# Modulation-map products on TensorE in four groups of 32 output partitions, in place of multiply-adds on VectorE

## The chip, the cores and the metric

The kernel runs on one core of one Trainium2 chip. The metric is the device time of one execution in microseconds, the median of several. The engines are called by the profile's names: PE is TensorE (PEld its weight loads), DVE is VectorE, ACT is ScalarE, SP is SyncE, on whose queue nearly all transfers are issued.

## The reference

One inference step of a two-layer backbone over 512 latent and 128 context tokens of 1024 features. Each layer is a feed-forward sub-layer, a token mixer (attention in layer 0, a gated recurrence in layer 1) and a second feed-forward sub-layer. Each of these sub-layers is shifted, scaled and gated by vectors that come from a linear map of a conditioning vector; this map is what the change touches:

```
mod_ctx_all = jnp.einsum('d,lde->le', jax.nn.silu(c_ctx), w_mod) + b_mod
mod_lat_all = jnp.einsum('bd,lde->lbe', jax.nn.silu(c), w_mod) + b_mod[:, None]
# w_mod: (2 layers, 1024, 9 * 1024)
...
mod = mod_lat_all[l].reshape(Bs, N_MOD, D_MODEL)
x = ffn_sublayer(x, mod, 0, norm_g[l, 0], norm_g[l, 1], ffn_w_in[l, 0], ffn_w_out[l, 0])
# ada_pre: rmsnorm(x, g) * (1 + scale) + shift;  ada_post: x + res_w * gate * rmsnorm(y, g)
```

So two vectors of 1024 (latent and context) are multiplied with 2 x 1024 x 9216 weights.

## The kernel before

All activations are held transposed, features on partitions, tokens on the free axis, in two groups g of 320 tokens. The main products run in `run_jobs` (L301): a job is one block of 128 output features over up to eight 128-deep steps, for one or both groups. Every weight is split into a high and a low part (`convert`, L241: ACT copies at L249, DVE subtracts at L250), and each step issues per group two 128x320 matmuls at L315 and one at L320. Weights arrive in three raw buffers (`ensure_dma`, L226, issued at L231 on SP's queue).

Everything else is written as Python generators in the list `bg`. `step_bg` (L281) advances the first of them by one `yield`; `run_jobs` calls it in slots between the steps of a job and once after it, so a generator's work is spread between main matmuls, and the number of its yields fixes its place in the program. The program is then given to a planner of the tile framework, which orders the instructions of each engine by priority (that is, program order) and by when it believes their inputs ready, and places all semaphore waits. It can draw an instruction forward where it believes the engine idle.

The modulation map is computed in 36 blocks of 512 columns. `startup` (L641) makes four of them (0 to 3) with products at L722; the other 32 are made by `mod_gen` (L599), run as a generator in three feed-forward stages: 12 blocks in the first sub-layer of layer 0 (gap 2), 12 in its second (gap 2), 8 in the first of layer 1 (gap 3), as `ffn_jobs` is called in `plan`. A block's weights come in two halves of 512 rows (`mod_load`, L554, issued at L559, two buffers named wmod, one DMA of 1 MB each).

In `mod_gen` before, for each of the eight 128-row steps k and each of the two vectors s, DVE multiplies a 128x512 tile by the scalar `CV[:, k, s]` and adds it into `macc` (L614 for k = 0, L616 for the others), with `gap` yields ahead of each. After step 3 and step 7 the load of the next block's half is issued. Then four matmuls (L626) of 128x256 with a column of ones sum `macc` over the partitions into four groups of 32 output partitions of an accumulator bank (`aux_tile`, two buffers of 128x1024), with the one column placed so that block i falls into rows 2i and 2i+1. ACT copies (i = 0, L631) or DVE adds (L633) the result into `ms`, and after the last block `mod_fin` (L562) brings it into place with four matmuls against `sel` (L567).

In `startup` a block is instead made by eight matmuls of the 128x32 slice of `CS` (zeros but for the two vectors in columns 2 and 3) with 128x512 of the weights, step k into output group k % 4, accumulating over halves and two blocks (L722).

Between sub-layers `chain_gen` (L469) runs the statistics and normalisations that hand one over to the next, on DVE and ACT, with small matmuls at L365 and L377; it uses the same two accumulator buffers.

Of the kernel before, what the change touches and what calls it, by code (L numbers as in the profile page):

```python
# [9 lines left out]
F32 = mybir.dt.float32  # L10
# [3 lines left out]
AF = mybir.ActivationFunctionType  # L14
ALU = mybir.AluOpType
# [4 lines left out]
KT = D // 128  # L20
# [129 lines left out]
class Net:  # L150
# [25 lines left out]
    def setup(self):  # L176
        tc, ctx = self.tc, self.ctx
        P = lambda n, b, **k: ctx.enter_context(tc.tile_pool(name=n, bufs=b, **k))
        self.const = P("const", 1)
        self.big = P("big", 1)  # L180
        self.rawp = P("rawp", RAW_BUFS)
        self.hlp = P("hlp", HL_BUFS)
        self.np_ = P("nrm", 3)
        self.small = P("small", 2)
        self.aux = P("aux", 2, space=PSUM)
        self.mm = P("mm", 1, space=PSUM)
        self.lane = 0
        self.in_attn = False
        big = self.big
        self.Y = [big.tile([128, KT, NG], F32, name="Y0"), None]  # L190
        self.X = big.tile([128, KT, NTOK], F32, name="X")
        self.H = big.tile([128, 2, KT, NTOK], F32R, name="H")
        c = self.const
        self.ident = c.tile([128, 128], F32, name="ident")
        self.sel = c.tile([128, 3, 32], F32, name="sel")
        self.CV = c.tile([128, KT, 2], F32, name="CV")
        self.one = c.tile([128, 64], F32, name="one")
        self.ones = c.tile([128, 1], F32, name="ones")
        self.MODF = c.tile([128, DEPTH * NMOD * KT, 2], F32, name="MOD")
        self.MOD = self.MODF.rearrange("p (l n) s -> p l n s", l=DEPTH)  # L200
        self.NGt = c.tile([128, 96], F32, name="NGt")
        self.BM = c.tile([128, 144], F32, name="BM")
        self.DT = c.tile([128, 50], F32, name="DT")
        self.PRE = c.tile([128, DEPTH, 3, KT, 2], F32, name="PRE")
        self.POST = c.tile([128, DEPTH, 3, KT, 2], F32, name="POST")
        self.acc = {}
        for g in range(2):
            self.acc[g] = c.tile([128, NG], F32, name=f"acc{g}")
        self.lam = c.tile([128, 1], F32, name="lam")
        self.lb = c.tile([128, 2, 16], F32, name="lb")  # L210
        self.again = c.tile([128, 1], F32, name="again")
# [370 lines left out]
    def mod_derive(self, l, p, k0=0, k1=KT):  # L582
# [11 lines left out]
        else:  # L594
            nc.vector.scalar_tensor_tensor(
                out=self.POST[:, l, j, k0:k1], in0=m, scalar=1.0 if j == 1 else 0.5, in1=gv, op0=ALU.mult, op1=ALU.mult
            )

    def mod_gen(self, first, n, gap):  # L599
        nc = self.nc  # L600
        ms = self.mod_p.tile([128, 256], F32, name="ms", tag="ms")
        ts = [self.mod_load(first, h) for h in range(2)]
        for _ in range(MOD_DELAY):
            yield
        for i in range(n):
            acc = [self.mod_p.tile([128, 512], F32, name="macc", tag=f"macc{s}") for s in range(2)]
            for k in range(KT):
                w = ts[k // 4][:, k % 4, :]
                for s in range(2):
                    for _ in range(gap):  # L610
                        yield
                    cv = self.CV[:, k, s:s + 1]
                    if k == 0:
                        nc.vector.tensor_scalar(out=acc[s], in0=w, scalar1=cv, scalar2=None, op0=ALU.mult)  # L614
                    else:
                        nc.vector.scalar_tensor_tensor(  # L616
                            out=acc[s], in0=w, scalar=cv, in1=acc[s], op0=ALU.mult, op1=ALU.add
                        )
                if k % 4 == 3 and i + 1 < n:
                    ts[k // 4] = self.mod_load(first + i + 1, k // 4)  # L620
            yield
            ps = self.aux_tile()
            for g in range(4):
                h, s = divmod(g, 2)
                o = 32 - (2 * i + s)
                nc.tensor.matmul(  # L626
                    out=ps[g * 32:(g + 1) * 32, 0:256], lhsT=self.one[:, o:o + 32],
                    rhs=acc[s][:, h * 256:(h + 1) * 256], start=True, stop=True, skip_group_check=True,
                )
            if i == 0:  # L630
                nc.scalar.activation(out=ms, in_=ps[:, 0:256], func=AF.Copy)  # L631
            else:
                nc.vector.tensor_tensor(out=ms, in0=ms, in1=ps[:, 0:256], op=ALU.add)  # L633
            yield
        yield
        self.mod_fin([(first, n)], ms, self.aux_tile(), True)
        for p in range(first // 2, (first + n) // 2):
            self.mod_derive(*divmod(p, NMOD))
        yield

    def startup(self):  # L641
        nc = self.nc
# [3 lines left out]
        self.open("start", "right", st_p=1)  # L646
        self.open("gs", "left", gs_p=1)
        S = self.st_p
        CS = S.tile([128, KT, 34], F32, name="CS")
        nc.sync.dma_start(out=self.ident, in_=A["k_ident"])  # L650
        rows = {}
        for nm, n in (("D", 50), ("A", 96), ("B", 72), ("C", 72)):
# [12 lines left out]
        for tb in range(5):  # L665
# [4 lines left out]
            src = A["x_sample"][0, tb * 128:(tb + 1) * 128, :] if tb < 4 else A["x_prompt"][0]  # L670
            nc.sync.dma_start(out=t, in_=src)
            xs.append(t)
        nc.vector.memset(CS, 0.0)
        nc.vector.memset(self.one, 0.0)
        nc.vector.memset(self.one[:, 32:33], 1.0)
        nc.vector.memset(self.ones, 1.0 / D)
        loads = []
        for c in (0, 2):
            ts = [self.gs_p.tile([128, 4, 512], F32, name=f"wm{c}{h}") for h in range(2)]
# [3 lines left out]
        ts = [y.rearrange("p k t -> p (k t)")[:, 0:2048].rearrange("p (k c) -> p k c", c=512) for y in self.Y]  # L683
        loads.append([self.mod_load(3, h, ts[h]) for h in range(2)])
        self.ensure_dma(RAW_BUFS - 1)
        ps = self.aux_tile()
# [3 lines left out]
            out=self.CV.rearrange("p k s -> p s k"),  # L690
            in_=self.DT[:, 32:48].rearrange("p (s k) -> p s k", s=2), func=AF.Silu,
        )
        nc.vector.tensor_copy(CS[:, :, 2:4], self.CV)
        ps = self.aux_tile()
        nc.tensor.transpose(ps[:, 0:96], rows["A"], self.ident[0:96, 0:96])
        nc.tensor.transpose(ps[:, 128:200], rows["B"], self.ident[0:72, 0:72])
# [3 lines left out]
        for kt in range(KT):  # L700
            ps = self.aux_tile()
# [8 lines left out]
            out=self.again, in0=self.DT[:, 48:49], scalar1=1.0 - LAM_INIT, scalar2=None, op0=ALU.mult  # L710
        )
        for half in range(2):
            if half == 0:
                for g in BOTH:
                    next(self.first_gens[g])
            ms = self.Y[half].rearrange("p k t -> p (k t)")[:, 2048:2560]
            ps = self.bank()
            for i in range(2):
                ts = loads[2 * half + i]
                for k in range(KT):  # L720
                    g = k % 4
                    nc.tensor.matmul(  # L722
                        out=ps[g * 32:(g + 1) * 32, :], lhsT=CS[:, k, 2 - 2 * i:34 - 2 * i],
                        rhs=ts[k // 4][:, k % 4, :], start=(i == 0 and k < 4), stop=(i == 1 and k >= 4),
                        skip_group_check=True,
                    )
            nc.scalar.activation(out=ms, in_=ps[:, 0:512], func=AF.Copy)
            if half == 0:
                for g in BOTH:
                    for _ in range(STAT_GAP):  # L730
                        next(self.first_gens[g])
            self.mod_fin([(half, 1), (2 + half, 1)], ms, self.bank(), False)
            self.mod_derive(0, 1, 4 * half, 4 * half + 4)
# [688 lines left out]
```

## Time and profile before

| what | value |
|---|---|
| median of 3 runs | 2908.82 us (2905.07 to 2910.05) |
| profiled execution | span 2910.1 us, its own time by the slowest run 2910.05 us |
| PE busy | 2855.3 us, 98%, 19278 matmul records |
| PEld busy | 2749.4 us, 94% |
| DVE busy | 1738.7 us, 60% |
| ACT busy | 995.4 us, 34% |
| DMA | 278.06 MB, mean 96 GB/s |
| mean granted TensorE clock | 0.989 of full speed |

The page gives busy times of one profiled execution. PE's matmuls overlap in their pipeline, so its busy time counts when it has any work; the distance between the starts of matmuls tells its speed. A matmul of two fp32 operands is recorded as two matmuls; the main ones at L315 and L320 use the split form and are one record each. A granted clock of 1.00 is 2.4 GHz and 0.50 is 1.2 GHz.

### The profile page before, as it was taken

Reading aid. Unit: us, or ns where it says so; the run is one execution under the profiler, and the core shown is the slowest. Engines: PE = TensorE matmul, PEld = TensorE weight load, DVE = VectorE, ACT = ScalarE, POOL = GpSimd, SP = SyncE. Lnnn points to the kernel's source line nnn. Section 1 sums busy time; section 2 is a strip of 40 time slices with the busy share of each in tenths; the row PEclk is TensorE's granted clock in tenths of the full one; section 3 lists DMA queues with packets and bytes.
Section 4 is the critical chain, followed back from the end, with each engine's and each line's share of the span. In section 5 each row is a group of like instructions: output and inputs, shape, how many; then the busy total and the mean of one; then the engine's idle time right before and its main releaser. Section 6 shows DMA issues by size and latency. Waiting matters only on the chain.

```text
span 2910.1 us, 46502 instructions
## 1 busy us (share of the span) xinstructions
PE 2855.3 (98%) x19278; PEld 2749.4 (94%) x19278; DVE 1738.7 (60%) x3605; ACT 995.4 (34%) x1949; POOL 0.2 (0%) x4
## 2 busy tenths in 40 slices
PE   7999999999999999999999999999999999999998
PEld 5999999888888999999999999999999999999998
DVE  6755645866677855665773554387677677223334
ACT  4222123455564422212332212243333344222233
POOL 0000000000000000000000000000000000000000
PEclk9999999999999999999999999999999999999999
DMA  8544432211113344454233433321121122222231
GB/s 264 169 152 139 137 106 81 59 34 36 44 50 101 95 139 151 124 159 138 80 115 104 130 104 107 89 60 55 55 59 51 55 61 80 80 80 73 79 87 39
DMA packets 424399, 278.06 MB, mean 96 GB/s; under 512 B 8410, under 2 KB 385788, under 8 KB 424188
## 3 DMA queue, kind: packets, MB, share of 16 engines
q1 hardware_dynamic: 423680, 274.89, 31.5%
q8 instruction: 152, 2.49, 0.3%
q14 instruction: 59, 0.48, 0.1%
q10 hardware_dynamic: 508, 0.20, 0.0%
HBM read 270.34 MB, written 4.72 MB: 95 GB/s over the span
## 4 chain that ended last, share of the span: by engine, by line
PE 91%; DVE 4%; ACT 2%; issue 1%; DMA 1%; ACTq 0%; DVEq 0%; SPq 0%
PE mmps L315 53%; PE mmps L320 26%; PE aux L1258 2%; PE aux L1067 2%; PE aux L1065 1%; PE mmps L1097 1%; PE aux L377 1%; PE aux L626 1%; PE mmps L1086 1%; ACT sq L1329 1%; PE aux L1295 0%; PE aux L365 0%; DVE whl L250 0%; DVE acc L399 0%; DVE rs_a L358 0%
## 5 line engine op out<-in xcount | busy, mean ns | idle before, releaser
L315 PE MATMUL mmps<-H,whl 128*128 128x320 f32 x7232 | 1447.0, 313 | 8.3 <-ACT H L454 6.1
L315 PEld LDWEIGHTS mmps<-H,whl 128*128 128x128 f32 x7232 | 1159.9, 189 | 26.1 <-issue 8.0
L320 PE MATMUL mmps<-H,whl 128*128 128x320 f32 x3616 | 898.0, 312 | 0.3 <-DVE whl L250 0.3
L250 DVE TENSOR_TENSOR whl<-wraw,whl 128x1024 fp32r<-128x1024 f32 (+1 forms) x324 | 387.7, 1197 | 424.0 <-ACT whl L249 422.7
L320 PEld LDWEIGHTS mmps<-H,whl 128*128 128x128 f32 x3616 | 626.3, 189 | 3.0 <-DVE whl L250 0.6
L249 ACT ACTIVATE whl<-wraw 128x1024 fp32r<-128x1024 f32 (+1 forms) x324 | 335.7, 1038 | 594.5 <-issue 369.0
L315 PE MATMUL mmps<-G,whl 128*128 128x320 f32 x2368 | 467.8, 311 | 1.2 <-ACT G L1343 1.2
L315 PEld LDWEIGHTS mmps<-G,whl 128*128 128x128 f32 x2368 | 378.2, 188 | 6.1 <-issue 3.3
L616 DVE SCALAR_TENSOR_TENSOR macc<-wmod,CV,macc 128x512 f32<-128x512 f32 x448 | 307.6, 746 | 0.0
L320 PE MATMUL mmps<-G,whl 128*128 128x320 f32 x1184 | 294.3, 310 | 0.0
L315 PE MATMUL mmps<-G,H 128*128 128x320 f32 x960 | 216.5, 312 | 0.0
L748 ACT ACTIVATE sa<-mmps 128x320 f32<-128x320 f32 x176 | 69.1, 435 | 427.9 <-PE mmps L320 427.8
L753 DVE TENSOR_TENSOR gm<-sa,mmps 128x320 f32<-128x320 f32 x176 | 79.2, 484 | 217.2 <-PE mmps L320 216.5
L320 PEld LDWEIGHTS mmps<-G,whl 128*128 128x128 f32 x1184 | 204.5, 188 | 0.1
L315 PEld LDWEIGHTS mmps<-G,H 128*128 128x128 f32 x960 | 160.7, 188 | 0.5
L320 PE MATMUL mmps<-G,H 128*128 128x320 f32 x480 | 149.7, 312 | 0.0
L837 DVE TENSOR_TENSOR Y<-Y,mmps 128x320 f32<-128x320 f32 x144 | 66.7, 484 | 133.3 <-PE mmps L320 133.3
L315 PE MATMUL mmps<-H,G 128*128 128x320 f32 x448 | 103.4, 312 | 0.0
L835 ACT ACTIVATE Y<-mmps 128x320 f32<-128x320 f32 x96 | 38.5, 435 | 180.3 <-PE mmps L320 180.0
L399 DVE TENSOR_TENSOR acc<-acc,sq 128x320 f32<-128x320 f32 x168 | 80.2, 487 | 20.3 <-ACT sq L398 18.9
L320 PEld LDWEIGHTS mmps<-G,H 128*128 128x128 f32 x480 | 90.3, 188 | 0.4
L997 DVE TENSOR_REDUCE sm<-aux 128x1 f32<-128x640 f32 x64 | 52.7, 824 | 53.9 <-PE aux L1067 53.8
(222 smaller groups left out, 2540.3 us busy)
## 6 DMA issues: line engine op xcount, KB each, us to landing
wraw<-in_ffn_w_in SPq DMA_DIRECT2D x192, 512.0 KB, 3.9
wmod<-in_w_mod SPq DMA_DIRECT2D x66, 1024.0 KB, 5.6
wraw<-in_ffn_w_out SPq DMA_DIRECT2D x64, 448.0 KB, 3.9
wraw<-in_hgrn_w_in SPq DMA_DIRECT2D x40, 512.0 KB, 3.9
wraw<-in_ffn_w_out SPq DMA_DIRECT2D x32, 512.0 KB, 4.1
wraw<-in_attn_w_in SPq DMA_DIRECT2D x24, 512.0 KB, 4.0
wm<-in_w_mod SPq DMA_DIRECT2D x4, 1024.0 KB, 11.5
wraw<-in_attn_w_out SPq DMA_DIRECT2D x8, 512.0 KB, 4.1
```

The source lines that it names most:

```text
L249: nc.scalar.activation(out=u.w[0][:, 0:nk, :], in_=u.raw[:, 0:nk, :], func=AF.Copy)
L250: nc.vector.tensor_tensor(out=u.w[1][:, 0:nk, :], in0=u.raw[:, 0:nk, :], in1=u.w[0][:, 0:nk, :].bitcast(F32), op=ALU.subtract)
L315: nc.tensor.matmul(out=ps[g][:, 0:NG], lhsT=w[0][:, a, :], rhs=rhs[:, r, b, g * NG:(g + 1) * NG], start=(i == 0 and r == 0), stop=False,)
L320: nc.tensor.matmul(out=ps[g][:, 0:NG], lhsT=w[1][:, a, :], rhs=rhs[:, 0, b, g * NG:(g + 1) * NG], start=False, stop=(i == last),)
L399: return lambda: nc.vector.tensor_tensor(out=acc, in0=acc, in1=sq, op=ALU.add)
L616: nc.vector.scalar_tensor_tensor(out=acc[s], in0=w, scalar=cv, in1=acc[s], op0=ALU.mult, op1=ALU.add)
L748: nc.scalar.activation(out=st[g], in_=ps, func=AF.Silu)
L753: nc.vector.tensor_tensor(out=t, in0=st[g], in1=ps, op=ALU.mult)
L837: nc.vector.tensor_tensor(out=y, in0=y, in1=ps, op=ALU.add)
L997: nc.vector.tensor_reduce(out=sm[:, c:c + 1], in_=x, axis=AX.X, op=ALU.max)
L1067: nc.tensor.matmul(out=o, lhsT=QL[r, qc], rhs=KH[r, c, k0:k1], start=False, stop=True)
L1258: nc.tensor.matmul(out=ps[:, c * 128:(c + 1) * 128], lhsT=km[:, c * 128:(c + 1) * 128], rhs=self.view(Q2, c * 128, dims), start=True, stop ...
```

## The change

`mod_gen` no longer uses DVE for the products. It builds its own `CS` (62 columns per step k, zeros but for the two vectors in columns 30 and 31), and for each half of a block, after 8 x gap yields, issues four matmuls of 128x512 into the four groups of 32 output partitions of one accumulator bank (`mod_rows`); the second half accumulates onto the first. The slice of `CS` shifts by two columns a block, so that block i falls into rows 2i and 2i+1. The load of the next block's half follows each half's products. `ms` is 512 columns wide instead of 256, and `mod_fin` selects sums of all four groups. The number of yields of a block stays the same (16 x gap + 2). `startup` uses the same helpers; the tile of ones (`one`) goes, and the memset of `CS` there is issued after the transposed vectors are at hand.

```diff
-        self.one = c.tile([128, 64], F32, name="one")
...
+    def mod_vectors(self, CS):
+        self.nc.vector.memset(CS, 0.0)
+        self.nc.vector.tensor_copy(CS[:, :, 30:32], self.CV)
+
+    def mod_rows(self, ps, CS, ts, i, half, first, last):
+        for k in range(4 * half, 4 * half + 4):
+            g = k % 4
+            self.nc.tensor.matmul(
+                out=ps[g * 32:(g + 1) * 32, 0:512], lhsT=CS[:, k, 30 - 2 * i:62 - 2 * i], rhs=ts[half][:, g, :],
+                start=first and half == 0, stop=last and half == 1, skip_group_check=True,
+            )
+
     def mod_gen(self, first, n, gap):
         nc = self.nc
-        ms = self.mod_p.tile([128, 256], F32, name="ms", tag="ms")
+        ms = self.mod_p.tile([128, 512], F32, name="ms", tag="ms")
+        CS = self.mod_p.tile([128, KT, 62], F32, name="CS", tag="CS")
+        self.mod_vectors(CS)
         ts = [self.mod_load(first, h) for h in range(2)]
         for _ in range(MOD_DELAY):
             yield
         for i in range(n):
-            acc = [self.mod_p.tile([128, 512], F32, name="macc", tag=f"macc{s}") for s in range(2)]
-            for k in range(KT):
-                w = ts[k // 4][:, k % 4, :]
-                for s in range(2):
-                    for _ in range(gap):
-                        yield
-                    cv = self.CV[:, k, s:s + 1]
-                    if k == 0:
-                        nc.vector.tensor_scalar(out=acc[s], in0=w, scalar1=cv, scalar2=None, op0=ALU.mult)
-                    else:
-                        nc.vector.scalar_tensor_tensor(
-                            out=acc[s], in0=w, scalar=cv, in1=acc[s], op0=ALU.mult, op1=ALU.add
-                        )
-                if k % 4 == 3 and i + 1 < n:
-                    ts[k // 4] = self.mod_load(first + i + 1, k // 4)
-            yield
-            ps = self.aux_tile()
-            for g in range(4):
-                h, s = divmod(g, 2)
-                o = 32 - (2 * i + s)
-                nc.tensor.matmul(
-                    out=ps[g * 32:(g + 1) * 32, 0:256], lhsT=self.one[:, o:o + 32],
-                    rhs=acc[s][:, h * 256:(h + 1) * 256], start=True, stop=True, skip_group_check=True,
-                )
+            for half in range(2):
+                for _ in range(8 * gap):
+                    yield
+                if half == 0:
+                    ps = self.aux_tile()
+                self.mod_rows(ps, CS, ts, i, half, True, True)
+                if i + 1 < n:
+                    ts[half] = self.mod_load(first + i + 1, half)
+            yield
             if i == 0:
-                nc.scalar.activation(out=ms, in_=ps[:, 0:256], func=AF.Copy)
+                nc.scalar.activation(out=ms, in_=ps[:, 0:512], func=AF.Copy)
             else:
-                nc.vector.tensor_tensor(out=ms, in0=ms, in1=ps[:, 0:256], op=ALU.add)
+                nc.vector.tensor_tensor(out=ms, in0=ms, in1=ps[:, 0:512], op=ALU.add)
             yield
         yield
-        self.mod_fin([(first, n)], ms, self.aux_tile(), True)
+        self.mod_fin([(first, n)], ms, self.aux_tile(), False)
...
-        CS = S.tile([128, KT, 34], F32, name="CS")
+        CS = self.mod_p.tile([128, KT, 62], F32, name="CS", tag="CS")
...
-        nc.vector.memset(CS, 0.0)
-        nc.vector.memset(self.one, 0.0)
-        nc.vector.memset(self.one[:, 32:33], 1.0)
...
-        nc.vector.tensor_copy(CS[:, :, 2:4], self.CV)
+        self.mod_vectors(CS)
...
             for i in range(2):
-                ts = loads[2 * half + i]
-                for k in range(KT):
-                    g = k % 4
-                    nc.tensor.matmul(
-                        out=ps[g * 32:(g + 1) * 32, :], lhsT=CS[:, k, 2 - 2 * i:34 - 2 * i],
-                        rhs=ts[k // 4][:, k % 4, :], start=(i == 0 and k < 4), stop=(i == 1 and k >= 4),
-                        skip_group_check=True,
-                    )
+                for h in range(2):
+                    self.mod_rows(ps, CS, loads[2 * half + i], i, h, i == 0, i == 1)
```

## Rows read from the trace of the kernel before

**Rows 1.** The page, part 1: busy time, share of the span, instructions.
```profile
PE 2855.3 (98%) x19278; PEld 2749.4 (94%) x19278; DVE 1738.7 (60%) x3605; ACT 995.4 (34%) x1949; POOL 0.2 (0%) x4
```

**Rows 2.** The page, part 4: the chain that ended last, by engine.
```profile
PE 91%; DVE 4%; ACT 2%; issue 1%; DMA 1%; ACTq 0%; DVEq 0%; SPq 0%
```

**Rows 3.** Table of stretches: busy us (instructions) by engine, granted clock, DMA share, GB/s.
```profile
37.50:39.10 1.60, 1.60 (x9) 0.20 (x8) 1.60 (x3) 0.09 (x1) 0.00 (x0) 0.59 1.05 372
957.00:963.80 6.80, 5.56 (x21) 5.13 (x21) 6.52 (x23) 3.55 (x7) 0.00 (x0) 0.50 0.33 84
...
1050.00:1350.00 300.00, 300.00 (x2073) 294.55 (x2072) 182.08 (x280) 69.31 (x116) 0.00 (x0) 1.00 0.47 143
2500.00:2800.00 300.00, 300.00 (x2047) 300.00 (x2047) 83.76 (x117) 69.75 (x117) 0.00 (x0) 1.00 0.26 76
```

**Rows 4.** Table of stretches for L315, then L320, each in both: PE, PEld busy.
```profile
1050.00:1350.00 300.00, 250.42 (x1334) 208.77 (x1334) 1.00 0.47 143
2500.00:2800.00 300.00, 255.33 (x1365) 213.94 (x1365) 1.00 0.26 76
...
1050.00:1350.00 300.00, 151.76 (x667) 111.21 (x666) 1.00 0.47 143
2500.00:2800.00 300.00, 155.32 (x682) 114.08 (x682) 1.00 0.26 76
```

**Rows 5.** Groups by line and shape: busy us, mean ns of one, idle before.
```profile
L616 DVE SCALAR_TENSOR_TENSOR macc<-wmod,CV,macc 128x512 f32<-128x512 f32 x448 | 307.6, 746 | 0.0
...
L626 PE MATMUL aux<-macc,one 128*32 128x256 f32 x256 | 21.7, 391 | 0.0
```

**Rows 6.** Timeline of PE around one L626 group: start us, duration us, line, operation.
```profile
87.94 0.31 PE L320 MATMUL mmps<-H,G 128*128 128x320 f32 x1
88.17 0.64 PE L626 MATMUL aux<-macc,one 128*32 128x256 f32 x8
88.74 0.56 PE L315 MATMUL mmps<-H,whl 128*128 128x320 f32 x2
89.14 0.31 PE L320 MATMUL mmps<-H,whl 128*128 128x320 f32 x1
```

**Rows 7.** Timeline of PE and its weight loads in the start-up.
```profile
18.46 1.06 PE L722 MATMUL mmps<-wm,CS 128*32 128x512 f32 x8
19.45 1.66 PE L703 MATMUL aux<-ident,xin 128*128 128x128 f32 x10
...
37.54 1.66 PE L722 MATMUL mmps<-wmod,CS 128*32 128x512 f32 x8
39.13 0.41 PE L315 MATMUL mmps<-H,whl 128*128 128x320 f32 x1
...
41.44 0.31 PE L320 MATMUL mmps<-H,whl 128*128 128x320 f32 x1
41.67 1.07 PE L722 MATMUL mmps<-wmod,CS 128*32 128x512 f32 x8
42.56 1.90 PE L722 MATMUL mmps<-Y,CS 128*32 128x512 f32 x16
...
42.99 0.13 PEld L722 LDWEIGHTS mmps<-Y,CS 128*32 128x32 f32 x4 [0.30 <-issue]
```

**Rows 8.** Timeline at a hand-over: PE's two waits (in brackets), DVE shortly before.
```profile
950.27 0.74 DVE L616 SCALAR_TENSOR_TENSOR macc<-wmod,CV,macc 128x512 f32<-128x512 f32 x1
...
955.73 0.80 PE L365 MATMUL aux<-ones,acc 128*128 128x1 f32 x6 [3.37 <-DVE rs_a L359]
...
958.94 1.63 PE L315 MATMUL mmps<-H,whl 128*128 128x320 f32 x4 [1.24 <-ACT H L454]
```

**Rows 9.** SP's waits (us, times, longest), and landing of the loads at L559.
```profile
SPq L559 <- DVE macc L616: 143.0, 53, 10.1
...
DMA to landing us min/median/max: 5.0/5.8/13.6
```

**Rows 10.** Instructions of the line that clears CS: duration ns min/median/max, start.
```profile
L673 DVE MEMSET CS<- x1: 285/285/285, 0.9 to 0.9; 128x272 f32 x1
```

## The prediction

> **What bounds the kernel now.** I read the page's busy shares first [rows 1]: TensorE (PE) is busy 98% of the span, VectorE (DVE) 60%. The chain of waits says the same of the path [rows 2]: 91% of it is PE, 4% DVE. Busy time of pipelined matmuls overlaps, so I checked with counts. The table of stretches [rows 3] has one in which the modulation work runs (1050 to 1350 us) and one in which there is none (2500 to 2800 us). In both PE is busy for all 300 us at full clock. In the second, every one of the 2047 matmuls is a 128x320 one of the main products (1365 + 682, [rows 4]), so one starts every 300 / 2047 = 146.6 ns. In the first there are 1334 + 667 = 2001 of them [rows 4]; at 146.6 ns they fill 293.3 us, and the 72 records of L626, nine groups of eight, are left with 6.7 us, 0.74 us a group. So in the modulation stretch there is no time in which PE waits for anybody, and DVE, busy 182 of 300 us, doesn't slow the main matmuls. Whatever is added to PE there lengthens the kernel by itself.
>
> **What is removed on DVE.** The multiply-adds of L616 go, 448 of 746 ns, 307.6 us of busy time [rows 5], and the first products of L614. All lie beside a full PE, so I take nothing for them. The bound above zero: DVE ends PE's waits only where one sub-layer hands over to the next, and some multiply-adds of the second modulation run were issued early, into the hand-over before 960 us. There PE idles 3.37 us and then 1.24 us with L616 still on DVE shortly before [rows 8], and the granted clock is 0.50, which is 1.2 GHz, for 6.8 us around its end [rows 3]; at 2.4 GHz that stretch would shrink by at most half, 3.4 us. All of it together is 8.0 us, the most that a lighter DVE can give back.
>
> **What is removed on PE.** Per block of 512 columns the four sums over partitions (L626, 256 columns, eight records) go. In the timeline of one group [rows 6] a main matmul starts at 87.94, the group at 88.17, the next main matmul at 88.74 and the third at 89.14: 1.20 us for three main steps, which need 0.44 us, so 0.76 us a group. That agrees with the 0.74 from the counts; I take 0.76. There are 256 / 8 = 32 groups [rows 5], 12 + 12 + 8 blocks.
>
> **What is added on PE.** Each block now has two groups (half 0 and half 1) of four products, 128x512 to 32 outputs each. The start-up has just this operation, L722, in this shape and with such operands [rows 7]. A group of eight records (each product in fp32 is recorded twice) started at 18.46 and the next operation at 19.45: 0.99 us. Within a row of groups, one pass of four takes 0.43 us (42.56 to 42.99), so 0.86 us is the two passes and the rest is the end of the group. Ahead of it stands the border from a main matmul, 0.23 us (41.44 to 41.67), the same as before L626 (87.94 to 88.17). Behind it the first two main matmuls take 0.40 us instead of 0.29 [rows 6], the re-entry. A half by this is 0.23 + 0.99 + 0.40 - 0.44 (three main steps) = 1.18 us. The 8 x gap yields between the halves put main matmuls between them, so both borders are paid twice a block: 2.36 us.
>
> Per block 2.36 - 0.76 = 1.60 us; 32 blocks: **+51.2 us**. The bounds of this term: without any border 2 x 0.86 - 0.76 = 0.96 us, +31 us; with the group at the low clock, 1.59 us from 37.54 to 39.13 [rows 7] at a granted clock of 0.59 [rows 3], a half is 1.78 and the sum +90 us. I stand by the middle value: the modulation stretches have a granted clock of 1.00 with L626 in them [rows 3], and L626 pays its borders there.
>
> The start-up rows say that the four groups run at once: the 0.43 us of a pass of four is two times 512 columns at 2.4 GHz, which one product alone would need. The Trainium skill ("TensorE: Matmul & The Clock Gate", Measured speedup vs the span model) speaks against this: it gives three column groups of 32 outputs and 512 columns a speedup of 2.38, not 3. Scaled to 3.2 for four, an estimate from that page, a pass would be 0.54 us, and the kernel 14 us slower than by the rows. The traced pass doesn't show that loss.
>
> **What is moved, and the small terms.** The weight-map loads (L559) keep their yield positions, but a buffer comes free when PE has read it, not DVE, and it is PE that waits if the data is late. Behind the load on SP's queue stand the loads of the main weights (L231). Before, SP waited for L616 53 times, 143.0 us in all, 10.1 us at the longest, and a load landed in 5.8 us, 13.6 at the longest [rows 9]. A half is read again one block later, about 31 us (nine groups in 300 us, some more), so even both longest together leave 7 us. I take 0. If a product is late, everything on PE behind it waits.
>
> The vectors CS are now set up three times more: a memset of 496 columns, where 272 took 285 ns [rows 10], so about 0.5 us, and a small copy, on DVE at the start of a feed-forward stage. In the steady stretches DVE's free time hides that; at a start without that cover it is at most 0.7 us each. I take 0 (bound +2). The copy and the addition of the map are twice as wide (512 for 256 columns); DVE loses far more than it gets, so nothing. The final selection has four matmuls as before. The accumulator bank is now held for half a block instead of about a microsecond, and the hand-overs use the same two buffers; in the code's order they are over before a block begins. If one had to wait, the nearest row is the 3.37 us stall [rows 8], twice at most (+7). The first block of the second and third run may also be put into a hand-over's idle time (-1.6 each).
>
> **Sum.** The profiled execution has a span of 2910.1 us, 1.3 us above the median of 2908.82. 2910.1 + 51.2 = 2961.3; against the median 2960.0.
>
> **Rivals.**
> 1. The halves run back to back. The code order has other matmuls between them, but the order on the engine is made by a planner, which may draw them together. Then one border and one re-entry a block go: 2.36 falls by 0.23 + 0.11 + (0.99 - 0.86) - 0.15 = 0.32 us, 10 us in all: 2950. Against it: PE is never idle in those stretches, so nothing calls the second half forward.
> 2. The hand-over gains: products fill PE's idle time before 960 us, DVE is lighter and the clock doesn't fall. At most the 8.0 us above, so 2952. For it: multiply-adds lie on DVE there [rows 8]. Against it: the chain there also goes through conversions and statistics that stay.
> 3. Late loads: PE takes over a wait that DVE could afford. 0.8 us exposed a block would be 25 us, 2985. Against it: 7 us in hand at the worst.
> 4. The four groups overlap worse than in the start-up, because in the modulation stretch they read memory beside conversions and loads. If only three ran at once, a pass would be 4/3 of 0.43 us, a half 0.28 us longer, 64 halves 18 us: 2978. Against it: L626 reads beside the same traffic, and its groups cost the same by counts over nine of them as in one timeline. The skill's page above points this way, with a smaller loss.
> 5. Not slower: PE only looks full in the modulation stretches, and DVE's traffic to memory stretches every main matmul there; without L616 they speed up. The price: a block holds 2001 / 9 = 222 main matmuls, so 1.60 us is won back from 7.2 ns each. If they went down to 133.3 ns (320 columns at 2.4 GHz), a block would gain 222 x 13.3 = 2.95 us, 1.35 net, and the kernel would take 2866. Against it: in the stretch without any modulation work the step is the same 146.6 ns, and with 0.76 us a group the step in the other comes out at (300 - 6.8) / 2001 = 146.5. I see no path to the 7.2 ns.
>
> **How the numbers follow.** Forecast 0.72; halves together 0.08; hand-over gains 0.08; late loads 0.05; worse overlap 0.04; not slower 0.03. The range goes from 2946 (rivals 1 or 2, with the first blocks hidden) to 2972 (the forecast with the small terms at their upper bounds, +9, and a few loads late by a microsecond). Within 0.2%, 5.8 us, is about what a measurement of this kernel can't tell from no change. Faster by more 0.02, within 0.02, slower 0.96: all cases but the last are slower.
>
> **What would show it.** In the changed profile the stretches with modulation work have PE busy for all their time at clock 1.00 and, for 300 us, about nine times 1.60 us fewer main matmuls: some 1903 to 1910 instead of 2001. Two groups of eight L722-like records stand in each block, each some 1.23 us from the main matmul before to the one after. DVE's busy time falls by some 310 us and buys nothing. The stages without modulation keep their lengths. Wrong would be: a step below 146 ns in the modulation stretches (rival 5), main matmuls missing between the halves (1), PE waiting for wmod (3), a pass longer than 0.43 us (4), or a hand-over shorter by several microseconds (2).

## The result, and the profile after

The changed kernel takes 2957.96 us (median of 4, 2955.59 to 2960.74) against 2909.44 us before (median of 4), a ratio of 1.0163 with a 95% interval of 1.0149 to 1.0178. It is slower, by 48.5 us between medians. Run again beside the experiments, it took 2956.15 us against 2913.07, a ratio of 1.0153 (1.0139 to 1.0167), 43.1 us. The profiled executions lie 43.7 us apart (2953.8 and 2910.1 us of span). A span lies 1.8 us below its execution's own time (2955.59 for the one of after); by the same 1.8 us the profiled execution of before is the one of 2911.89 us, which the median ahead of the prediction did not yet hold. Times of single executions scatter by some 7 us.

In the changed file the main matmuls are at L314 and L319 (L315 and L320 before), the modulation products at L605, the statistics at L364 (L365 before). The page of after, parts 1 and 4:

```profile
PE 2905.0 (98%) x19534; PEld 2751.9 (93%) x19534; DVE 1433.9 (49%) x3097; ACT 997.0 (34%) x1949; POOL 0.2 (0%) x4
...
PE 92%; DVE 4%; ACT 2%; issue 1%; DMA 1%; ACTq 0%; DVEq 0%; SPq 0%
```

Against [rows 1] DVE lost 304.8 us of work and PE gained 49.7 us of busy time; the chain's shares [rows 2] hardly moved. The same stretches as in [rows 3], all instructions (columns as there):

```profile
1050.00:1350.00 300.00, 300.00 (x2046) 280.40 (x2045) 83.62 (x118) 65.18 (x110) 0.00 (x0) 1.00 0.43 133
2500.00:2800.00 300.00, 300.00 (x2047) 300.00 (x2046) 86.32 (x119) 73.20 (x121) 0.00 (x0) 1.00 0.27 78
```

and, of the first stretch, L314, L319 and L605 by themselves (PE, then PEld):

```profile
1050.00:1350.00 300.00, 238.06 (x1263) 197.18 (x1263) 1.00 0.43 133
...
1050.00:1350.00 300.00, 143.62 (x631) 105.32 (x630) 1.00 0.43 133
...
1050.00:1350.00 300.00, 20.25 (x152) 2.99 (x152) 1.00 0.43 133
```

Both stretches are full on PE at a clock of 1.00, as before. DVE's busy time in the modulation stretch has halved (182.08 to 83.62 us), but the number of main matmuls in 300 us fell from 2001 [rows 4] to 1263 + 631 = 1894; 19 groups of L605 (152 / 8) stand in their place. Timeline of PE around one of them, to be held against [rows 6]:

```profile
141.50 0.46 PE L319 MATMUL mmps<-H,whl 128*128 128x320 f32 x2
141.88 1.06 PE L605 MATMUL aux<-wmod,CS 128*32 128x512 f32 x8
142.88 0.85 PE L314 MATMUL mmps<-H,whl 128*128 128x320 f32 x4
143.56 0.45 PE L319 MATMUL mmps<-H,whl 128*128 128x320 f32 x2
```

The second L319 starts one step after 141.50, at 141.64; the group begins at 141.88, 0.24 us later; 142.88 is 1.00 us after that, and the first two main matmuls behind it take 0.39. In the shape of the prediction's sum this is 0.24 + 1.00 + 0.39 - 0.44 = 1.19 us. With it the step of the main matmuls is (300 - 19 x 1.19) / 1894 = 146.5 ns, the same as without modulation.

That the four products of a group run at once is seen in the first block of the first run, which the planner split into three groups. The first of them holds one product alone (two records):

```profile
58.81 1.05 PE L605 MATMUL aux<-wmod,CS 128*32 128x512 f32 x2
59.79 0.55 PE L314 MATMUL mmps<-H,whl 128*128 128x320 f32 x2
```

From its start to the next main matmul are 0.98 us, against 1.00 for the group of four products above.

The loads: SP's wait for the buffers, now for PE, and their landing at L558:

```profile
SPq L558 <- PE aux L605: 204.9, 56, 11.1
```

```profile
DMA to landing us min/median/max: 5.0/5.6/14.2
```

Against [rows 9] SP waits longer for them, 204.9 us in all instead of 143.0, and 11.1 instead of 10.1 at the longest (beside a single wait of 28 us for another matmul, which stands in both traces); no row of PE's waits names wmod. The longest landings, 13.6 and 14.2 us, are those of loads of the start-up; into the wmod buffers it was 9.9 us at most before and 10.5 after.

Where in the kernel the time went is read from the starts of the same main matmul in both traces; each has 16512 of them, in order of time, counted from 0 here. The difference of start times (after minus before, us) at some of them:

| main matmul | start before | difference | since the row above |
|---|---|---|---|
| 200 (after the start-up and the first block's products) | 75.2 | +1.8 | +1.8 |
| 2800 (first run of 12 blocks done) | 466.5 | +18.7 | +16.9 |
| 4600 (attention done) | 936.3 | +17.2 | -1.5 |
| 4800 (hand-over to the second stage) | 976.4 | +10.3 | -7.0 |
| 8000 (second run done) | 1463.8 | +29.8 | +19.5 |
| 11200 (third run, 8 blocks, done) | 1950.7 | +42.0 | +12.2 |
| 16511 (the last) | 2896.5 | +43.7 | +1.7 |

In the steady modulation stretches the difference grows by 1.61 us a block. Outside them it moves by some 1.5 us in the attention and behind the third run, and at one place by more: 7.0 us are won between 936 and 976 us. In a second trace of the changed kernel (the first run of the next section) the two small steps read +1.3 and -1.6, so they are scatter, and the 7.0 is the same. The stretch there after the change:

```profile
950.00:985.00 35.00, 35.00 (x239) 34.17 (x238) 30.34 (x83) 19.96 (x38) 0.00 (x0) 1.00 0.26 75
```

PE has no idle time in it and the clock is 1.00; the waits of 3.37 and 1.24 us and the stretch at 0.50 ([rows 8], [rows 3]) are gone. So the change costs what was forecast and gives back something that was not in the sum.

### The profile page after: what moved, and what is told of

Same layout as the page of the kernel before. It is cut to its first block, busy times and chain, and to the rows that moved or that the text cites. A ratio compares the mean times of both kernels' runs of the same rounds, so it can differ in the third digit from the quotient of the medians.

```text
span 2953.8 us, 46482 instructions
## 1 busy us (share of the span) xinstructions
PE 2905.0 (98%) x19534; PEld 2751.9 (93%) x19534; DVE 1433.9 (49%) x3097; ACT 997.0 (34%) x1949; POOL 0.2 (0%) x4
## 4 chain that ended last, share of the span: by engine, by line
PE 92%; DVE 4%; ACT 2%; issue 1%; DMA 1%; ACTq 0%; DVEq 0%; SPq 0%
PE mmps L314 52%; PE mmps L319 26%; PE aux L1247 2%; PE aux L605 2%; PE aux L1056 2%; PE aux L1054 1%; PE mmps L1086 1%; PE aux L376 1%; PE mmps L1075 1%; ACT sq L1318 1%; PE aux L1284 0%; PE aux L364 0%; DVE whl L249 0%; DVE acc L398 0%; DVE rs_a L357 0%
## 5 line engine op out<-in xcount | busy, mean ns | idle before, releaser
L314 PE MATMUL mmps<-H,whl 128*128 128x320 f32 x7232 | 1447.5, 313 | 5.8 <-ACT H L453 3.7
L314 PEld LDWEIGHTS mmps<-H,whl 128*128 128x128 f32 x7232 | 1157.7, 189 | 51.1 <-issue 34.0
L319 PE MATMUL mmps<-H,whl 128*128 128x320 f32 x3616 | 897.5, 312 | 0.0
L319 PEld LDWEIGHTS mmps<-H,whl 128*128 128x128 f32 x3616 | 625.7, 189 | 3.2 <-DVE H L461 0.8
L314 PE MATMUL mmps<-G,whl 128*128 128x320 f32 x2368 | 467.6, 311 | 1.2 <-ACT G L1332 1.2
L314 PEld LDWEIGHTS mmps<-G,whl 128*128 128x128 f32 x2368 | 376.7, 188 | 16.4 <-issue 12.6
L319 PE MATMUL mmps<-G,whl 128*128 128x320 f32 x1184 | 293.5, 309 | 0.0
L314 PE MATMUL mmps<-G,H 128*128 128x320 f32 x960 | 216.4, 312 | 0.0
L319 PEld LDWEIGHTS mmps<-G,whl 128*128 128x128 f32 x1184 | 203.9, 188 | 0.1
L314 PEld LDWEIGHTS mmps<-G,H 128*128 128x128 f32 x960 | 160.7, 188 | 0.5
L319 PE MATMUL mmps<-G,H 128*128 128x320 f32 x480 | 149.7, 312 | 0.0
L314 PE MATMUL mmps<-H,G 128*128 128x320 f32 x448 | 103.4, 312 | 0.0
L824 ACT ACTIVATE Y<-mmps 128x320 f32<-128x320 f32 x96 | 38.5, 435 | 184.0 <-PE mmps L319 183.6
L319 PEld LDWEIGHTS mmps<-G,H 128*128 128x128 f32 x480 | 90.3, 188 | 0.3
L744 ACT ACTIVATE G<-gm 128x320 fp32r<-128x320 f32 x176 | 73.4, 456 | 31.9 <-DVE gm L742 31.9
L745 DVE TENSOR_TENSOR G<-gm,G 128x320 fp32r<-128x320 f32 x176 | 79.4, 485 | 5.6 <-ACT G L744 5.2
```

The source lines that it names most:

```text
L314: nc.tensor.matmul(out=ps[g][:, 0:NG], lhsT=w[0][:, a, :], rhs=rhs[:, r, b, g * NG:(g + 1) * NG], start=(i == 0 and r == 0), stop=False,)
L319: nc.tensor.matmul(out=ps[g][:, 0:NG], lhsT=w[1][:, a, :], rhs=rhs[:, 0, b, g * NG:(g + 1) * NG], start=False, stop=(i == last),)
L744: nc.scalar.activation(out=hi, in_=t, func=AF.Copy)
L745: nc.vector.tensor_tensor(out=self.tv(self.G[:, 1, jj, :], g), in0=t, in1=hi.bitcast(F32), op=ALU.subtract)
```

## The experiments

**What the added and removed groups cost.** The changed kernel once more, then three kernels measured beside it.

> The changed kernel once more, beside the three below, as their common base. 2953 to 2961 us. In its trace each half's group lay 1.23 us from main matmul to main matmul and cost 1.19 us, 64 of them; the hand-over before 960 us was 7.0 us shorter than before the change.

Measured: 2956.15 us (2953.42 to 2961.24), span 2953.6. Its trace wins 7.0 us at the same hand-over.

First, the products of the second half of each block left out (the added last argument, whose lines are not shown, lets the first half end its sum):

```diff
-                self.mod_rows(ps, CS, ts, i, half, True, True)
+                if half == 0:
+                    self.mod_rows(ps, CS, ts, i, half, True, True, True)
```

> The changed kernel with the products of the second half of each block (rows 512 to 1023 of the weights) left out; loads, additions and yields stay. Theory (each group costs PE 1.19 us that nothing hides): 32 x 1.19 = 38 us faster than the changed kernel, 2919 us. Rival (part of the 48 us is not PE's groups but something else that came with the change, wider additions, the set-up of the vectors, buffers freed later): less than 30 us faster, above 2927 us.

Measured: 2917.66 us (median of 8, 2913.31 to 2927.06), 38.5 us below the changed kernel where 38 were expected. Between the profiled executions (spans 2918.3 and 2953.6 us) it is 35.3, and in the steady stretch of the first run 1.19 us a group left out. So the groups carry the cost; with single executions of this kernel 14 us apart, a rest of a few microseconds that comes from something else would not show.

Second, both halves back to back:

```diff
             for half in range(2):
-                for _ in range(8 * gap):
-                    yield
                 if half == 0:
+                    for _ in range(16 * gap):
+                        yield
                     ps = self.aux_tile()
```

> The changed kernel with both halves of a block issued back to back after 16 x gap yields; nothing is left out. Theory (the cost is passes plus two borders a group): one border and one re-entry a block go, 0.32 to 0.35 us of 2.38, so 10 to 11 us faster than the changed kernel, about 2947 us. Rival (all of the cost is in the passes of the fp32 products, borders are hidden): no change, 2957 us.

Measured: 2946.92 us (2945.58 to 2950.34), 9.2 us below the changed kernel. Timeline of PE around one block of it:

```profile
108.79 0.46 PE L319 MATMUL mmps<-H,whl 128*128 128x320 f32 x2
109.18 1.93 PE L605 MATMUL aux<-wmod,CS 128*32 128x512 f32 x16
111.03 0.85 PE L314 MATMUL mmps<-H,whl 128*128 128x320 f32 x4
111.72 0.45 PE L319 MATMUL mmps<-H,whl 128*128 128x320 f32 x2
```

From 109.18 to 111.03 are 1.85 us for sixteen records, against 2 x 1.00 us for two groups of eight; with the borders ahead and behind, a block is 0.24 + 1.85 + 0.40 - 0.44 = 2.05 us instead of 2.38. Before rounding the difference, one border with its re-entry, is 0.32 us. In the first block of each run the planner again split or joined the groups as in the changed kernel, so 29 blocks save it: 9.3 us, against the 9.2 measured. In the other 29 blocks the halves of the changed kernel are therefore not drawn together by the planner, and they pay for it.

Third, from the kernel before, the sums over partitions (and with them their additions into `ms`) left out but for the first and last block of each run:

```diff
             yield
+            if 0 < i < n - 1:
+                yield
+                continue
             ps = self.aux_tile()
```

> The kernel before with the sums over partitions (L626) left out for all but the first and the last block of each run, 26 of 32 groups, so the map is only partly computed; the multiply-adds stay. Theory (a group costs 0.76 us of PE's time): 26 x 0.76 = 20 us faster than before, 2890 us. Rival (the old groups were partly hidden, so that the change's difference per block is not 2.38 - 0.76): less than 12 us faster.

Measured: 2888.20 us (median of 5, 2884.93 to 2895.28) against 2913.07, a ratio of 0.9920 (0.9906 to 0.9934): 24.9 us faster between medians, 19 to 27 by the interval, 20 expected. Its profiled execution has a span 17.4 us below that of before, and in its steady modulation stretches 7.6 us for every ten groups left out, 0.76 each. The old groups were not hidden either.

**What the relieved DVE gives.** Two kernels, both made from the one before, so without any work added on PE.

```diff
                     if k == 0:
                         nc.vector.tensor_scalar(out=acc[s], in0=w, scalar1=cv, scalar2=None, op0=ALU.mult)
-                    else:
-                        nc.vector.scalar_tensor_tensor(
-                            out=acc[s], in0=w, scalar=cv, in1=acc[s], op0=ALU.mult, op1=ALU.add
-                        )
```

> The kernel before with the 448 multiply-adds of L616 left out (only the first product of each block and vector stays; so the modulation vectors are only partly computed). It has DVE's relief without the added work on PE. Theory (PE is the limit in the modulation stretches, DVE is off the path there, and only the hand-over before 960 us can gain): 2901 to 2909 us, the step of the main matmuls stays 146.6 ns, every gain lies before the start of the second feed-forward stage. Rival (DVE's work or traffic stretches the main matmuls): 30 us or more faster, 2880 or below, the step falls below 146 ns in the modulation stretches.

Measured: 2904.38 us (median of 8) against 2911.62 (median of 23 for these four), a ratio of 0.9978 (0.9968 to 0.9988), about 7 us faster. The stretch from 1050 to 1330 us of it, all instructions, then its L315 and L320:

```profile
1050.00:1330.00 280.00, 280.00 (x1936) 274.56 (x1935) 86.27 (x134) 63.44 (x105) 0.00 (x0) 1.00 0.46 142
...
1050.00:1330.00 280.00, 233.35 (x1242) 194.57 (x1243) 1.00 0.46 142
...
1050.00:1330.00 280.00, 141.60 (x622) 103.57 (x620) 1.00 0.46 142
```

and the same three of the kernel before:

```profile
1050.00:1330.00 280.00, 280.00 (x1937) 274.55 (x1936) 170.95 (x265) 64.11 (x107) 0.00 (x0) 1.00 0.46 141
...
1050.00:1330.00 280.00, 233.43 (x1244) 194.55 (x1243) 1.00 0.46 141
...
1050.00:1330.00 280.00, 141.30 (x621) 103.58 (x621) 1.00 0.46 141
```

DVE's work is halved, and PE does 1864 main matmuls in place of 1865 in the same time. Rival 5 of the prediction is out: with 84.7 us less on DVE nothing got faster there. All of its gain of some 7 us lies elsewhere; the starts of main matmuls put 7.0 us between the 4600th and the 4800th, as in the changed kernel (and 2.8 us of its one trace into the attention, where two traces of the changed kernel differ by as much).

The second ties the scalars of the second modulation run to a result of that stage, so that its multiply-adds can't be drawn ahead into the hand-over; all work is done:

```diff
             nc.scalar.activation(out=st[g], in_=ps, func=AF.Silu)
+            if (l, s, g) == (0, 1, 1) and not st.get("tied"):
+                st["tied"] = True
+                nc.vector.scalar_tensor_tensor(
+                    out=self.CV2.rearrange("p k s -> p (k s)"), in0=st[g][:, 0:16], scalar=0.0,
+                    in1=self.CV.rearrange("p k s -> p (k s)"), op0=ALU.mult, op1=ALU.add,
+                )
...
-                    cv = self.CV[:, k, s:s + 1]
+                    cv = (self.CV2 if first == 16 else self.CV)[:, k, s:s + 1]
```

> The kernel before, with the scalars of the second modulation run tied to a result of that stage's head (g = 1, first block), so that none of its multiply-adds can be drawn ahead into the hand-over; nothing is left out. Theory A (the multiply-adds on DVE in the hand-over before 960 us made the two PE waits of 3.37 and 1.24 us and the low clock behind them, and the changed kernel's gain of 7 us there is their absence): 2902 to 2906 us, these waits and the 6.8 us at 1.2 GHz gone. Theory B (the gain there came from another order of the conversions, or from chance between executions): 2907 to 2912 us, the waits still there or moved.

Measured: 2905.03 us (median of 10) against 2911.62, a ratio of 0.9977 (0.9968 to 0.9987). The hand-over, in the tied kernel and in the one before (all engines, clock third from the end):

```profile
930.00:970.00 40.00, 40.00 (x273) 39.16 (x272) 35.23 (x96) 23.52 (x45) 0.00 (x0) 1.00 0.23 67
```

```profile
930.00:970.00 40.00, 35.40 (x225) 34.17 (x224) 37.06 (x102) 18.75 (x38) 0.00 (x0) 0.91 0.39 119
```

273 matmuls in place of 225, no idle PE, full clock. PE's statistics there no longer wait: of the tied kernel (its L366 and L378 are L365 and L377 before; a wait would stand in brackets, as in [rows 8]):

```profile
939.29 0.72 PE L366 MATMUL aux<-ones,acc 128*128 128x1 f32 x6
943.78 1.07 PE L378 MATMUL aux<-ident,rs_y 128*128 128x128 f32 x6
953.98 0.72 PE L366 MATMUL aux<-ones,acc 128*128 128x1 f32 x6
958.86 1.07 PE L378 MATMUL aux<-ident,rs_y 128*128 128x128 f32 x6
```

Theory A holds: with every multiply-add still there, only later, the 7 us come back, and no more is won by leaving them all out (7.2 us against 6.6). The gain of the changed kernel at this place needs no products on PE.

The traces also show where the chain was held up. Between a statistic on PE (L365) and the small matmuls that use it (L377) DVE works out a reciprocal square root in short steps, each waiting for the one before (L350 to L360). In the kernel before:

```profile
924.54 0.83 PE L365 MATMUL aux<-ones,acc 128*128 128x1 f32 x6
930.35 0.16 DVE L358 TENSOR_TENSOR rs_a<-rs_y 128x3 f32<-128x3 f32 x1
930.42 0.75 DVE L616 SCALAR_TENSOR_TENSOR macc<-wmod,CV,macc 128x512 f32<-128x512 f32 x1
931.09 0.16 DVE L359 TENSOR_TENSOR rs_a<-rs_a,rs_h 128x3 f32<-128x3 f32 x1
934.99 0.97 PE L377 MATMUL aux<-ident,rs_y 128*128 128x128 f32 x6
```

and in the tied kernel:

```profile
921.39 0.83 PE L366 MATMUL aux<-ones,acc 128*128 128x1 f32 x6 [0.17 <-DVE acc L400]
924.80 0.97 PE L378 MATMUL aux<-ident,rs_y 128*128 128x128 f32 x6
```

Before, the planner had put nine multiply-adds (6.66 us) and two conversions between these steps, so that from L365 to L377 there are 10.45 us; in the tied kernel none, and there are 3.41, 7.0 us less. The same distance is 3.41 us in the changed kernel and 3.25 without multiply-adds. PE does not wait there yet, it has main matmuls left; its waits come from 952 us on [rows 8], as the delayed chain goes on. No run delayed this stretch alone, and without the multiply-adds the planner also ordered the other instructions anew, so that it makes up the whole 7.0 us is read from the traces and not shown by itself.

**A version that beats both.** If a group is mostly borders, two blocks can share one: the sums of a pair of blocks accumulate in one bank (with four more KB of `macc` in a pool of its own, opened after the start-up).

```diff
-            for g in range(4):
-                h, s = divmod(g, 2)
-                o = 32 - (2 * i + s)
...
+            if b != 1:
+                continue
+            yield
+            ps = self.aux_tile()
+            for e, acc in enumerate(accs):
+                for g in range(4):
+                    h, s = divmod(g, 2)
+                    o = 32 - (2 * (i - 1 + e) + s)
...
+                        rhs=acc[s][:, h * 256:(h + 1) * 256], start=(e == 0), stop=(e == 1),
```

> The kernel before with the sums over partitions (L626) of two blocks in one group of 16 records, accumulated in one bank; nothing is left out. If a group is 0.76 us of which the passes are 2 x 0.21 us and the rest is the two borders, a pair costs 0.76 + 0.43 instead of 1.52: 0.33 us less for each of 16 pairs, 5.3 us, 2904 us. If the borders don't matter (the cost is all passes): no change, 2909.

Measured: 2913.24 us (median of 11) against 2911.62, a ratio of 1.0005 (0.9996 to 1.0014): no gain. By the starts of main matmuls its profiled execution saves the 0.33 us a pair in the steady stretches, but loses 2.0 us again just after the hand-over (PE waits of 1.29 and 0.39 us at a place where the kernel before has none, below; six multiply-adds lie on DVE from 985 to 997 us, where the kernel before has none either) and 2.1 us in the attention stage. The trace is of an execution of 2909.88 us, 3.4 below the median, so it doesn't show all that keeps the pairs from a gain.

```profile
995.19 0.56 PE L315 MATMUL mmps<-H,whl 128*128 128x320 f32 x2 [1.29 <-ACT H L454]
996.43 0.42 PE L315 MATMUL mmps<-H,whl 128*128 128x320 f32 x1 [0.39 <-DVE H L462]
```

> The pairs and the tied second run together; nothing is left out. By theory A the two add up: 2897 to 2901 us. By theory B only the pairs count: about 2904 us.

Measured: 2900.99 us (median of 5, 2898.29 to 2904.79) against 2911.62, a ratio of 0.9963 (0.9951 to 0.9976). It is the fastest of those that do all the work, 10.6 us below the kernel before and 4.0 below the tied one, where pairs were to give 5.3 (its span is 5.9 us below that of the tied one). One group of a pair:

```profile
106.88 0.46 PE L321 MATMUL mmps<-H,whl 128*128 128x320 f32 x2
107.27 1.07 PE L634 MATMUL aux<-macc,one 128*32 128x256 f32 x16
108.27 0.85 PE L316 MATMUL mmps<-H,whl 128*128 128x320 f32 x4
108.95 0.45 PE L321 MATMUL mmps<-H,whl 128*128 128x320 f32 x2
```

0.24 + 1.00 + 0.40 - 0.44 = 1.20 us for two blocks, as expected, 0.60 a block against 0.76.

## Why the prediction was right, and where it was off

The time, 2957.96 us, is 2 us from the forecast of 2960.0 and the direction is as forecast. That it came so near is partly luck: between the two profiled executions the change costs 43.7 us, 7.5 less than the 51.2 of the sum. The median that the forecast was added to lay 3.1 us below the profiled execution of before, and the median after lies 2.4 us above the one of after, which makes up for most of it. By its steps:

- **What bounds the kernel:** right. PE is full in the modulation stretches before and after, its step doesn't depend on DVE (146.5 ns in both), and DVE's 300 us bought nothing there.
- **The removed sums, 0.76 us a group:** right; leaving them out gave 0.76 each in the trace.
- **The added products, 1.18 us a half:** right; 1.19 in the trace, 1.2 from the medians of the kernel with one half left out (38.5 / 32; 1.1 from the spans). The start-up's rows carried over to the steady stretches, the four groups overlap there as well (0.98 us for one product, 1.00 for four), so rival 4 is out. The smaller speedup that the Trainium skill gives for such column groups ("TensorE: Matmul & The Clock Gate", Measured speedup vs the span model) doesn't show in these traces.
- **Both borders paid twice:** right; joining the halves saved 9.2 us. Only the first block of each run differs: in the second and third run its halves were issued partly together, and in the first run it was split into three groups.
- **Per block +1.60 us, 51.2 in all:** 1.61 in the trace. The number of main matmuls in 300 us was put at 1903 to 1910 for nine blocks; it is 1894 with 19 groups, 9.5 blocks, in the stretch. A block of this stage holds 204 main matmuls and lasts 30.7 us before and 32.3 after, not a ninth of 300; rival 5's 222 main matmuls a block is too many for the same reason. Neither touches the forecast.
- **Late loads (rival 3):** didn't happen. The longest wait for a buffer that the products held was 11.1 us and the longest landing in one 10.5, together less than a block. (The 13.6 us that the prediction took for the landing is a load of the start-up.)
- **The lighter DVE, taken at 0 within bounds of 0 to 8.0 us:** this is the term that failed. It is 7.0 us, near its upper bound. The prediction set it up as a rival with a chance of 0.08 and an end of its own (2952), but it doesn't exclude the forecast, it adds to it: 32 blocks of 1.61 are 51.5; less the 7.0, and less 0.8 where the third run's first block hid in the next hand-over, that is the 43.7 between the two profiles. The argument against it, that conversions and statistics stay in that chain, was no measure of how late the multiply-adds made them: a reciprocal square root took 10.45 us from L365 to L377 where 3.41 are enough. The two comparisons of medians, +48.5 and +43.1, lie on either side of that, as far apart as single executions scatter.
- **Small terms:** the vectors' set-up took 0.47 us of DVE each and cost nothing that shows: at the 100th main matmul the changed kernel is 0.3 us ahead, and at the 134th, with the three groups of the first block between them, 1.7 us behind.

## What to carry to other kernels

Where one engine is full without a gap, price a change by what it adds to that engine in its own start-to-start times, borders included; the relief of another engine counts only at the places where the full one waits, and there it can be had without moving the work, by keeping it out of that place. In these traces each short group of another tile shape paid a border on PE, so gather them. And look on the helping engine for long instructions between the steps of a short chain that the full engine will wait for.

## What the runs showed of the hardware

A change from 128-column to four 32-column groups and back costs PE about 0.32 us beyond the passes (a block in two groups takes 2 x 1.188 us, joined 2.053), for groups of 256 columns (2 x 0.762 us against 1.200 for a pair) as for those of 512. Four fp32 products of 128x512 to 32 outputs run together: one alone held PE for 0.98 us up to the next main matmul, four for 1.00.

Between executions of one kernel the attention stage, in which PE is idle for some 11 of 460 us, runs at 1.2 GHz for different lengths of time, and some of the executions' scatter of a few us lies there. The first and the second profiled execution of the changed kernel have a mean granted clock of 0.97 and 0.96 from 480 to 940 us, and 2694 and 2675 matmuls:

```profile
480.00:940.00 460.00, 449.25 (x2694) 392.49 (x2694) 316.89 (x838) 249.69 (x585) 0.00 (x0) 0.97 0.19 55
```

```profile
480.00:940.00 460.00, 449.37 (x2675) 393.07 (x2674) 314.32 (x832) 247.63 (x582) 0.00 (x0) 0.96 0.19 54
```

One such stretch of the first, in which the granted clock is 0.50:

```profile
567.30:577.60 10.30, 7.71 (x27) 6.90 (x28) 8.45 (x33) 5.01 (x14) 0.00 (x0) 0.50 0.00 1
```
